# A two-layer hybrid step in split fp32: the high part against 512 columns per tile from layer 1's first down product on

## The chip, the cores and the metric

The kernel runs on 1 core of one Trainium2 chip. The metric is the device time of one execution in microseconds (us); before the change the median of 3 runs is 2454.88 us (2451.24 to 2457.85). PE is the matmul engine (PEld its weight loads), ACT the scalar engine, DVE the vector engine, POOL the general engine, SP the engine that issues most DMAs here.

## What is computed

Two layers over 128 context and 128 latent tokens (256 columns in all) with width 2048. Cut to what matters here:

```python
def trunk_layer(x, mod, ...):
    shift1, scale1, gate1, shift2, scale2, gate2 = mod      # mod = silu(c) @ w_mod + b_mod
    q_r, k_r, v_r, g_r, q_a, k_a, v_a = project(modulate(x, shift1, scale1), w_in_l)
    ...                                                     # retention heads and attention heads
    x = x + gate1 * (jnp.concatenate([y_r, y_a], axis=-1) @ w_out_l)
    x = x + gate2 * conv_ffn(modulate(x, shift2, scale2), w_up_l, conv_w_l, conv_b_l, w_down_l)

def conv_ffn(h, w_up_l, conv_w_l, conv_b_l, w_down_l):      # D_FF = 5632, conv of width 3 over tokens
    up = jnp.pad(h @ w_up_l, ...)
    u = conv_b_l + sum(up[:, j:j + T] * conv_w_l[j] for j in range(3))
    gate, val = jnp.split(u, 2, axis=-1)
    return (jax.nn.silu(gate) * val) @ w_down_l
```

All weights are fp32 in DRAM and every one is read once.

## The kernel before

**Tiles, pieces, items.** Activations lie transposed, features on partitions, the 256 tokens in the free dimension. A weight is cut into tiles of 128 by 128; eight tiles are a piece, and the kernel is a list of 768 pieces in a fixed order: layer 0's input projection (pieces 0 to 87), its output projection `out` (88 to 119), then three thirds of the gated MLP, each an `up` product and a `down` product (120 to 383); layer 1 the same from 384, with its `out` at 472, its first `up` at 504 and its first `down` at 568. The thirds hold 16, 16 and 12 chunks of 128 hidden features. A group is four output chunks `n` of 128 features; an `up` chunk needs 16 tiles, a `down` chunk 16, 16 or 12.

**Split products.** To keep fp32 accuracy with single-pass fp32r matmuls, each weight piece is split on ACT into a rounded high part `hi` (L478) and on DVE into the rest `lo` (L479), three pieces ahead (`LOOK`), and each activation likewise: of the 512 columns of an `hT` chunk or of a `ypair` chunk the first 256 are the high part, the last 256 the low part. `triple` (L644 to L648) then makes three matmuls of 256 columns per tile into one accumulator: `hi` by high, `hi` by low, `lo` by high. Each matmul instruction loads its own weights.

**Accumulators.** `ps_m` holds five PSUM banks of 512 columns. Two output chunks share a bank (columns 0 to 255 and 256 to 511). When a pair is done, `evac` passes the bank on: for `up` to `ffn_pair` (convolution, silu, product, split; one stage per piece later), for `down` and `out` to ACT (times the gate, L726) and DVE (added to `xT`, L728). The last two chunks of `out` and of the last `down` take a bank each and go through `evac_one` (L700). In the first group of each `down` the four chunks are interleaved over all but the last four feature chunks.

**Modulation.** The vectors `shift`, `scale`, `gate` are products of `w_mod` (1 MB loads into the three `vec` buffers, in the order in which they are used) with two condition columns. Some are made on PE (`mod`, L402, four plain fp32 matmuls per load; `modq`, L388, one quarter of a vector in four loads), others as dot products on DVE (`dot`, L411, two instructions of 2.28 us per load). A plan made before the code is written out puts them behind pieces: `quota` with its `knots` for `mod`, `room`, `due` and `plan` for `dot`. Before, neither comes before piece 48 (`ahead`). Loads of pieces (`raw`, 512 KB, L335, five buffers) and of modulation (`vec`, L325) share SP's queue in order of their need.

**Side work.** The attention and retention heads of a layer are generators that `step_side` advances by one step behind each piece (and in the middle of it where two wait). An attention group (`q_task`) runs scores, softmax (`norm`), transposes on PE (`flip`, L857) and the product with the values (`mix`, L870) for three batches of heads.

## Time and profile before

| what | value |
|---|---|
| median of 3 runs | 2454.88 us (2451.24 to 2457.85) |
| the profiled execution, time | 2457.62 us |
| its span on the core | 2455.8 us, mean granted clock 0.99 |
| PE busy | 97% of the span, 19694 matmuls |
| PEld, DVE, ACT busy | 93%, 75%, 49% |
| DMA | 619 MB, mean 252 GB/s |

PE is busy in all but a few of the 40 slices. A matmul's start and end overlap with its neighbours', so its mean length (280 ns) is not what it costs; the distance from one start to the next is.

### The profile page before, as it was taken

The page shows a single profiled execution, that of the slowest core. Times are in us where ns is not written, and L with a number is a line of the kernel's source. Part 1 is how long each engine was busy: PE and PEld are TensorE (multiplying, and loading weights), DVE is VectorE, ACT ScalarE, POOL GpSimd, SP SyncE. Part 2 cuts the span into 40 slices and gives each one's busy share as a digit, 9 for nine tenths or more (in the row PEclk, how much of TensorE's full clock was granted, in tenths as well). Part 3 has the DMA queues.
Part 4 walks back from the last instruction along what each step waited for, and adds up shares of the span by engine and source line. Part 5 has one row for each costly group of instructions (what it writes and reads, how often), then busy time and mean ns, then how long its engine had stood idle before and what let it go on. Part 6 is the DMA issues. An engine that isn't in the chain of part 4 may idle for free.

```text
span 2455.8 us, 47593 instructions
## 1 busy us (share of the span) xinstructions
PE 2383.7 (97%) x19694; PEld 2287.2 (93%) x19694; DVE 1853.3 (75%) x2461; ACT 1203.4 (49%) x1901; POOL 21.7 (1%) x29
## 2 busy tenths in 40 slices
PE   6999999999999999999999999999999999999998
PEld 3888888889999999999989899999999999999997
DVE  4557778769998899889987777797896466655665
ACT  3534434455544455445556444456554445544554
POOL 0000000000000000000000000000000000000000
PEclk8999999999999999999999999999999999999999
DMA  9987788976888777777775677877676666666653
GB/s 377 350 310 258 274 308 327 372 252 230 277 277 283 264 254 271 274 268 256 254 285 191 231 275 280 298 269 257 227 253 187 183 188 186 186 182 186 188 181 121
DMA packets 146569, 619.46 MB, mean 252 GB/s; under 512 B 16304, under 2 KB 22448, under 8 KB 121392
## 3 DMA queue, kind: packets, MB, share of 16 engines
q1 hardware_dynamic: 138816, 605.24, 71.5%
q10 hardware_dynamic: 7536, 11.19, 1.3%
q8 instruction: 154, 2.52, 0.4%
q14 instruction: 63, 0.52, 0.1%
HBM read 611.64 MB, written 4.72 MB: 251 GB/s over the span
## 4 chain that ended last, share of the span: by engine, by line
PE 85%; DVE 8%; DMA 3%; issue 2%; ACT 2%; ACTq 0%; POOL 0%; DVEq 0%; SPq 0%; POOLq 0%
PE acc L646 27%; PE acc L648 26%; PE acc L647 26%; DVE lo L479 2%; DVE hua L411 2%; PE md L388 2%; DMA vec<-in_w_modq 2%; DMA vec<-in_w_mod 1%; PE md L402 1%; ACT hi L478 1%; ACT pr L842 0%; DMA vec<-in_w_dot 0%; DVE grp L640 0%; PE aux L870 0%; PE aux L443 0%
## 5 line engine op out<-in xcount | busy, mean ns | idle before, releaser
L646 PE MATMUL acc<-hT,hi 128*128 128x256 f32 x4224 | 1201.4, 284 | 5.9 <-ACT hT L573 5.9
L479 DVE TENSOR_TENSOR lo<-raw,hi 128x1024 fp32r<-128x1024 f32 x768 | 934.9, 1222 | 349.8 <-ACT hi L478 348.4
L648 PE MATMUL acc<-hT,lo 128*128 128x256 f32 x4224 | 1182.2, 280 | 2.4 <-DVE lo L479 2.4
L647 PE MATMUL acc<-hT,hi 128*128 128x256 f32 x4224 | 1182.2, 280 | 0.6 <-DVE hT L578 0.6
L478 ACT CAST hi<-raw 128x1024 fp32r<-128x1024 f32 x768 | 803.4, 1050 | 628.5 <-PE acc L647 543.9
L646 PEld LDWEIGHTS acc<-hT,hi 128*128 128x128 f32 x4224 | 795.9, 188 | 33.7 <-issue 15.3
L648 PEld LDWEIGHTS acc<-hT,lo 128*128 128x128 f32 x4224 | 796.0, 188 | 3.8 <-DVE lo L479 3.6
L647 PEld LDWEIGHTS acc<-hT,hi 128*128 128x128 f32 x4224 | 794.0, 188 | 4.2 <-issue 1.9
L648 PE MATMUL acc<-ypair,lo 128*128 128x256 f32 x1920 | 544.1, 283 | 2.3 <-DVE lo L479 2.3
L646 PE MATMUL acc<-ypair,hi 128*128 128x256 f32 x1920 | 546.1, 284 | 0.0
L647 PE MATMUL acc<-ypair,hi 128*128 128x256 f32 x1920 | 543.8, 283 | 0.0
L411 DVE SCALAR_TENSOR_TENSOR hua<-vec,cbc 128x2048 bf16<-128x2048 f32 x208 | 475.2, 2284 | 5.8 <-DMA vec<-in_w_dot 5.8
L646 PEld LDWEIGHTS acc<-ypair,hi 128*128 128x128 f32 x1920 | 369.0, 192 | 9.3 <-issue 6.7
L648 PEld LDWEIGHTS acc<-ypair,lo 128*128 128x128 f32 x1920 | 369.0, 192 | 3.0 <-DVE lo L479 3.0
L647 PEld LDWEIGHTS acc<-ypair,hi 128*128 128x128 f32 x1920 | 369.1, 192 | 0.1
L726 ACT ACTIVATE gx<-acc,modT 128x128 f32<-128x128 f32 x240 | 68.6, 369 | 113.5 <-PE acc L648 113.5
L728 DVE TENSOR_TENSOR xT<-gx,xT 128x512 f32<-128x512 f32 x60 | 41.5, 691 | 71.0 <-ACT gx L726 70.9
L755 DVE SCALAR_TENSOR_TENSOR cv<-acc,cst,cv 128x254 f32<-128x254 f32 x176 | 84.8, 482 | 6.2
L746 ACT ACTIVATE cv<-acc,cst 128x256 f32<-128x256 f32 x176 | 89.3, 558 | 0.0
L388 PE MATMUL md<-vec,sc 128*32 128x512 f32 x448 | 62.2, 664 | 26.5 <-DMA vec<-in_w_modq 26.5
L753 DVE SCALAR_TENSOR_TENSOR cv<-acc,cst,cv 128x254 f32<-128x254 f32 x176 | 83.5, 475 | 0.0
L759 ACT ACTIVATE cv<-cv 128x256 f32<-128x256 f32 x88 | 36.4, 414 | 71.3 <-DVE cv L755 71.2
(130 smaller groups left out, 893.9 us busy)
## 6 DMA issues: line engine op xcount, KB each, us to landing
raw<-in_w_up SPq DMA_DIRECT2D x352, 512.0 KB, 4.3
vec<-in_w_dot SPq DMA_DIRECT2D x104, 1024.0 KB, 5.3
raw<-in_w_in SPq DMA_DIRECT2D x176, 512.0 KB, 5.4
raw<-in_w_down SPq DMA_DIRECT2D x176, 512.0 KB, 4.2
vec<-in_w_modq SPq DMA_DIRECT2D x56, 1024.0 KB, 7.4
vec<-in_w_mod SPq DMA_DIRECT2D x32, 1024.0 KB, 8.3
raw<-in_w_out SPq DMA_DIRECT2D x64, 512.0 KB, 5.9
xT<-in_xT ACTq DMA_DIRECT2D x2, 1024.0 KB, 9.5
```

What stands on the lines that cost most here:

```text
L388: nc.tensor.matmul(md[0][32 * j:32 * j + 32, :], sc[:, 2 * kc:2 * kc + 32], t[:, 512 * i:512 * i + 512], start=kc < 4, stop=kc >= 12)
L411: nc.vector.scalar_tensor_tensor(hua.rearrange("p c t -> p (c t)").bitcast(BF16), raw[key], 1.0, acc[:, k, :], op0=ALU.mult, op1=ALU.mult, ...
L478: nc.scalar.copy(hi, r)
L479: nc.vector.tensor_tensor(lo, r, hi.bitcast(F32), op=ALU.subtract)
L646: nc.tensor.matmul(out, hi, src[:, 0:256], start=first, stop=False, skip_group_check=True)
L647: nc.tensor.matmul(out, hi, src[:, 256:512], start=False, stop=False, skip_group_check=True)
L648: nc.tensor.matmul(out, lo, src[:, 0:256], start=False, stop=last, skip_group_check=True)
L726: nc.scalar.activation(tv[:, i, P * s:P * s + P], pv[:, i, P * s:P * s + P], AF.Copy, scale=modT[l][:, v, nt + i, s:s + 1])
L728: nc.vector.tensor_tensor(xT[:, nt:nt + 2, :], tv, xT[:, nt:nt + 2, :], op=ALU.add)
L746: nc.scalar.activation(t, src, AF.Identity, bias=C("convb", l * 2 * FC + f, 1), scale=w)
L753: nc.vector.scalar_tensor_tensor(t[:, :, 1:P], src[:, :, 0:P - 1], w[0], t[:, :, 1:P], op0=ALU.mult, op1=ALU.add)
L755: nc.vector.scalar_tensor_tensor(t[:, :, 0:P - 1], src[:, :, 1:P], w[2], t[:, :, 0:P - 1], op0=ALU.mult, op1=ALU.add)
```

## The change

Three edits.

1. `halves(j, g)` holds for the `up` and `down` groups of layer 1 from its first `down` on (pieces 568 to 767, that is 896 `up` tiles and 704 `down` tiles). There a tile takes two matmuls in place of three: `hi` by all 512 columns (high and low activations) into a whole bank, and `lo` by the high 256 columns into the bank's first half. An output chunk thus has a bank of its own, and when it is complete ACT copies the bank's second half to SBUF (`tb`) and DVE adds the first half to it (`r`); `evac` and `evac_one` then read `r`.
2. Layer 0's plan: `mod` may start at piece 43 and has a knot at `out`'s start, three quarters of 32 loads by then; `dot` may also stand in pieces 27 to 31 and 43 to 47.
3. In `q_task` the first batch's `flip` has a step of its own behind the second batch's `norm`.

```diff
-    knots = [(ahead, 0), (gstart["up", 0] - 6, 2 * MU), (gstart["kv", 1] + 16, 2 * MU),
+    knots = [(ahead - 5, 0), (gstart["out", 0], 3 * MU // 2), (gstart["up", 0] - 6, 2 * MU), (gstart["kv", 1] + 16, 2 * MU),
...
-        if j >= ahead and not ends:
-            room[j] = DSHARE[g["kind"]] if j >= gstart["out", 0] else 0.3
+        if not ends:
+            if j >= gstart["out", 0]:
+                room[j] = DSHARE[g["kind"]]
+            elif j >= ahead or j >= 2 * WIDE and j % (2 * WIDE) >= 11:
+                room[j] = 0.3
...
-        elif issued[0] + 1 < quota(j, knots):
+        if j >= ahead - 5 and not hs and issued[0] + 1 < quota(j, knots):
...
+            if halves(j, g):
+                src = Y(kc) if g["kind"] == "down" else hT[:, kc, :]
+                if cur["ps"][n] is None:
+                    cur["ps"][n] = ps_m.tile([P, 512], F32, tag="m", name="acc")
+                out = cur["ps"][n]
+                c[n] += 1
+                nc.tensor.matmul(out, hi_t[j][:, P * i:P * i + P], src, start=c[n] == 1, stop=False,
+                                 skip_group_check=True)
+                nc.tensor.matmul(out[:, 0:256], lo_t[j][:, P * i:P * i + P], src[:, 0:256], start=False,
+                                 stop=c[n] == nk, skip_group_check=True)
+                if c[n] == nk:
+                    fin.append((n, out, single))
+                continue
...
-            if single:
+            if halves(j, g):
+                if n % 2 == 0:
+                    cur["r"] = tp.tile([P, 512], F32, tag="t2", name="r", bufs=4)
+                r = cur["r"][:, 256 * (n % 2):256 * (n % 2) + 256]
+                t = tp.tile([P, 256], F32, tag="t1", name="tb", bufs=3)
+                nc.scalar.copy(t, ps[:, 256:512])
+                nc.vector.tensor_tensor(r, ps[:, 0:256], t, op=ALU.add)
+                if single:
+                    evac_one(g, g["ns"][n], r)
+                elif n % 2 == 1:
+                    evac(gi, g, n, cur["r"])
+            elif single:
...
+    def halves(j, g):
+
+        return g["l"] == DEPTH - 1 and g["kind"] in ("up", "down") and g["first"] >= gstart["down", DEPTH - 1]
...
-        for step in ([(scores, 0)], [(scores, 1)], [(norm, 0)], [(norm, 1), (flip, 0)], [(scores, 2), (mix, 0)],
+        for step in ([(scores, 0)], [(scores, 1)], [(norm, 0)], [(norm, 1)], [(flip, 0)], [(scores, 2), (mix, 0)],
                      [(flip, 1), (norm, 2)], [(mix, 1)], [(flip, 2)], [(mix, 2)]):
```

On PE, at the second feature chunk of layer 1's first `down` group (the numbers behind the names tell banks and weight pieces apart), before:

```order
L646 MATMUL acc_21300<-ypair_19772,hi_21229 128x256
L647 MATMUL acc_21300<-ypair_19772,hi_21229 128x256
L648 MATMUL acc_21300<-ypair_19772,lo_21230 128x256
L646 MATMUL acc_21307<-ypair_19772,hi_21229 128x256
L647 MATMUL acc_21307<-ypair_19772,hi_21229 128x256
L648 MATMUL acc_21307<-ypair_19772,lo_21230 128x256
```

and at the same place now:

```order
L614 MATMUL acc_21300<-ypair_19772,hi_21229 128x512
L616 MATMUL acc_21300<-ypair_19772,lo_21230 128x256
L614 MATMUL acc_21303<-ypair_19772,hi_21229 128x512
L616 MATMUL acc_21303<-ypair_19772,lo_21230 128x256
L614 MATMUL acc_21306<-ypair_19772,hi_21229 128x512
L616 MATMUL acc_21306<-ypair_19772,lo_21230 128x256
L614 MATMUL acc_21309<-ypair_19772,hi_21229 128x512
L616 MATMUL acc_21309<-ypair_19772,lo_21230 128x256
```

Each tile has two instructions in place of three, and the group's four chunks lie in four banks instead of two; the whole program has 1600 matmuls fewer.

On SP, the loads issued towards the end of layer 0's `out` product (`raw` are weight pieces, `vec` modulation loads, by the DRAM array that they come from), before:

```order
L325 DMA vec<-in_w_mod 128x2048 x2
L335 DMA raw<-in_w_out 128x1024
L335 DMA raw<-in_w_up 128x1024
L325 DMA vec<-in_w_dot 128x2048
L335 DMA raw<-in_w_up 128x1024 x2
L325 DMA vec<-in_w_modq 128x2048 x3
L335 DMA raw<-in_w_up 128x1024
L325 DMA vec<-in_w_modq 128x2048
L335 DMA raw<-in_w_up 128x1024 x4
```

and now:

```order
L329 DMA vec<-in_w_dot 128x2048
L329 DMA vec<-in_w_mod 128x2048
L339 DMA raw<-in_w_out 128x1024
L329 DMA vec<-in_w_mod 128x2048
L339 DMA raw<-in_w_out 128x1024 x2
L339 DMA raw<-in_w_up 128x1024
L329 DMA vec<-in_w_modq 128x2048
L339 DMA raw<-in_w_up 128x1024 x2
L329 DMA vec<-in_w_modq 128x2048 x2
L339 DMA raw<-in_w_up 128x1024
L329 DMA vec<-in_w_modq 128x2048
```

The last `dot` load ahead of the first `modq` load has moved in front of the last two `mod` loads, and the first `modq` load stands two weight pieces sooner.

On ACT, in layer 0's first attention group (`pr` are the exponentials, `pt` the copy behind the transposes of `flip`, `ypair` the result of `mix`), before:

```order
L478 CAST hi<-raw 128x1024
L840 ACTIVATE st<-st 128x2
L842 ACTIVATE pr,st<-aux,st 128x256 x2
L478 CAST hi<-raw 128x1024
L859 COPY pt<-aux 128x512
L840 ACTIVATE st<-st 128x2
L842 ACTIVATE pr,st<-aux,st 128x256 x2
L876 CAST ypair<-aux 128x2x128 x2
```

and now:

```order
L482 CAST hi<-raw 128x1024
L872 ACTIVATE st<-st 128x2
L874 ACTIVATE pr,st<-aux,st 128x256 x2
L482 CAST hi<-raw 128x1024
L891 COPY pt<-aux 128x512
L482 CAST hi<-raw 128x1024
L872 ACTIVATE st<-st 128x2
L874 ACTIVATE pr,st<-aux,st 128x256 x2
L908 CAST ypair<-aux 128x2x128 x2
```

One weight piece's cast now stands between the first `flip` and the third batch's scores; the attention group has ten steps in place of nine.

## Rows read from the trace of the kernel before

**Rows 1.** the page of before: busy us, share of the span, instruction counts

```profile
PE 2383.7 (97%) x19694; PEld 2287.2 (93%) x19694; DVE 1853.3 (75%) x2461; ACT 1203.4 (49%) x1901; POOL 21.7 (1%) x29
```

**Rows 2.** stretches: length, busy (xcount) of PE, PEld, DVE, ACT; clock, DMA

```profile
390.00:520.00 130.00, 118.43 (x933) 101.42 (x932) 93.49 (x118) 52.10 (x94) 1.38 (x2) 0.96 0.93 352
1871.70:2441.80 570.10, 570.10 (x4802) 569.98 (x4800) 330.34 (x409) 285.32 (x435) 0.00 (x0) 1.00 0.58 179
1875.00:1960.00 85.00, 85.00 (x710) 85.00 (x710) 43.47 (x43) 38.97 (x60) 0.00 (x0) 1.00 0.60 182
1970.00:2050.00 80.00, 80.00 (x682) 80.00 (x681) 49.94 (x69) 40.35 (x56) 0.00 (x0) 1.00 0.62 188
```

**Rows 3.** groups of 1871.7 to the end: names, shapes, xcount | busy, mean ns

```profile
L646 PE MATMUL acc<-hT,hi 128*128 128x256 f32 x896 | 250.9, 280 | 0.0
L479 DVE TENSOR_TENSOR lo<-raw,hi 128x1024 fp32r<-128x1024 f32 x197 | 241.1, 1224 | 192.4 <-ACT hi L478 192.4
L478 ACT CAST hi<-raw 128x1024 fp32r<-128x1024 f32 x197 | 206.7, 1050 | 240.0 <-PE acc L647 210.6 <-ACT cv L746 24.5 <-issue 5.0
L646 PE MATMUL acc<-ypair,hi 128*128 128x256 f32 x704 | 199.2, 283 | 0.0
...
L753 DVE SCALAR_TENSOR_TENSOR cv<-acc,cst,cv 128x254 f32<-128x254 f32 x58 | 27.5, 475 | 0.0
L760 DVE TENSOR_TENSOR cv<-cv 128x256 f32<-128x256 f32 x29 | 12.1, 419 | 0.0
```

**Rows 4.** PE timeline, 12 matmuls apart, granted clock 0.5

```profile
517.53 0.41 PE L647 MATMUL acc<-hT,hi 128*128 128x256 f32 x1
...
520.09 0.41 PE L647 MATMUL acc<-hT,hi 128*128 128x256 f32 x1
```

**Rows 5.** PE timeline, nine matmuls apart, right after a wait

```profile
586.45 0.28 PE L647 MATMUL acc<-hT,hi 128*128 128x256 f32 x1
...
587.47 0.28 PE L647 MATMUL acc<-hT,hi 128*128 128x256 f32 x1
```

**Rows 6.** PE timeline, plain fp32 products of the side work at half clock

```profile
238.75 1.91 PE L828 MATMUL aux<-KT,grp 128*128 128x256 f32 x4
240.45 1.11 PE L870 MATMUL aux<-pt,vtok 128*128 128x512 f32 x2
```

**Rows 7.** PE timeline, the same products at full clock

```profile
1353.79 1.03 PE L828 MATMUL aux<-KT,grp 128*128 128x256 f32 x4
1354.65 1.02 PE L870 MATMUL aux<-pt,vtok 128*128 128x512 f32 x2
```

**Rows 8.** ACT by line: the one copy of this size out of a bank

```profile
L529 ACT COPY rb<-aux 128x256 f32<-128x256 f32 x5 | 1.9, 373 | 5.2 <-PE aux L528 5.2
```

**Rows 9.** what PE waited for, 200 to 520: us in total, times, longest

```profile
PE md L388 <- DMA vec<-in_w_modq: 6.1, 1, 6.1
PE md L402 <- DMA vec<-in_w_mod: 3.0, 2, 2.8
PE aux L857 <- ACT pr L842: 2.6, 1, 2.6
PE aux L857 <- DVE pr L850: 1.5, 2, 0.9
```

**Rows 10.** what PE waited for, 1230 to 1600

```profile
PE aux L857 <- DVE pr L850: 2.2, 1, 2.2
PE aux L857 <- ACT pr L842: 1.6, 1, 1.6
```

**Rows 11.** PE timeline, the wait at the end of the out product

```profile
495.09 1.93 PE L388 MATMUL md<-vec,sc 128*32 128x512 f32 x8 [6.09 <-DMA vec<-in_w_modq]
...
497.33 0.41 PE L647 MATMUL acc<-ypair,hi 128*128 128x256 f32 x1
...
499.68 0.41 PE L646 MATMUL acc<-ypair,hi 128*128 128x256 f32 x1
```

**Rows 12.** SP timeline, loads issued ahead of that wait

```profile
486.63 8.30 SPq L325 DMA_DIRECT2D vec<-in_w_modq  x3
```

More of the change, by code (lines that the diff above doesn't have):

```diff
@@ L149, in body @@
         gstart.setdefault((g["kind"], g["l"]), j)
+        g.setdefault("first", j)
     def mod_event():
@@ L600, in emit_piece @@
         fin = []
+        c = cur["n"]
         for i, (n, kc) in enumerate(p["tiles"]):
-            c = cur["n"]
             single = g["ns"][n] >= KC - 2 and last_add(g)
+            if halves(j, g):
[11 more added lines that the diff above has]
+                continue
             b = n if single else n // 2 * 2
```

## The prediction, made before the result was known

> **What bounds the kernel now.** I read the busy line first: PE is busy 97% of the span and has as many weight loads as matmuls [rows 1]; the load of its own weights goes with every matmul. Then the stretches: from 1871.7 to 2441.8, where layer 1's first down product begins and the last matmul ends, PE is busy for all 570.1 us at full clock, while DVE and ACT are busy 330 and 285 us and DMA 0.58 [rows 2]. So in the part that the change rewrites, the end is set by the distance of one matmul from the next, and by nothing else. That distance comes from the counts: 682 in 80 us of an up product and 710 in 85 us of a down product, two or three of each begun before the stretch, are 0.118 and 0.120 us [rows 2]. With the counts of the two forms [rows 3], 3 x (896 x 0.1178 + 704 x 0.120) = 570.0 us: the whole stretch. The mean length of 280 ns is that of overlapping instructions and costs nothing.
>
> The early part, layer 0's input and out products, is another regime: between 390 and 520 PE is busy 118 of 130 us with DMA at 0.93 [rows 2], and it waits by name for modulation loads and for the softmax [rows 9].
>
> **What a 512-column matmul costs.** This decides nearly all. At half clock (1.2 GHz) twelve matmuls take 2.56 us, 0.2133 each [rows 4]: exactly one column per cycle for 256 columns, nothing on top. At full clock (2.4 GHz) the same stream is 0.1067, but they start 0.118 or 0.120 apart: 11 to 13 ns on top. What adds them? Right after a wait nine of them went at 0.113 each [rows 5]. One and the same instruction at 0.113, 0.118 and 0.120 speaks against a slower rate per column, and for a hand-over between the weight load and the stream, which at full clock are about as long as each other. The trace has matmuls with a stream twice as long that load their own weights too: plain fp32 passes of the attention's scores take (240.45 - 238.75) / 4 = 0.425 at half clock [rows 6] and 0.215 at full clock [rows 7], only 2.5 ns above the half. Their stream is as long as that of 512 single-pass columns. So I take 0.215 for the new `hi` matmul; the `lo` matmul behind it is again 256 columns long with the next weight load beside it, and keeps 0.118 or 0.120.
>
> A tile then takes 0.333 us in up products (0.353 before) and 0.335 in down products (0.360 before). 896 x 0.020 + 704 x 0.025 = 35.5 us; I take 35 off the 570.
>
> Bounds: if the 11 and 13 ns belong to every fp32r matmul whatever its length, one of them is saved per tile: 896 x 0.0111 + 704 x 0.0133 = 19 us. If they are a rate per column, nothing is saved. The nearest rows, at the same stream length, are the 0.215 ones, so I take the upper end.
>
> The Trainium skill (page "TensorE: Matmul & The Clock Gate", section "Wait — 56ns, not 53.3ns?") has a fixed 2.5 ns per warm matmul at every length; by it alone 1600 matmuls fewer save 4 us. The 256-column matmuls here don't follow it, with 11 to 13 ns [rows 2]; the plain fp32 passes do, with 0.215 [rows 7].
>
> **What the halves add.** The 26 groups concerned have 104 output chunks; each now needs one ACT copy of 128x256 out of a bank, 0.373 us [rows 8], and one DVE addition, between 0.419 and 0.475 us [rows 3]. That is 39 us on ACT and 44 to 49 on DVE, beside PE: ACT goes to some 324 of 535 us and DVE to 377 of 535. Both stay below PE. They queue in order, though: behind each copy stands the next `hi` cast (1.05 us), behind each addition the next `lo` (1.22) [rows 3]. Those are made three pieces ahead, about 8 us, so 0.4 us in front of them is hidden by that lead; ACT's casts already wait 211 us for PE to give buffers back [rows 3]. Without the cover each chunk would cost PE 0.8 us.
>
> Banks: a chunk holds one of five. Between two uses of a bank lie four other chunks, 16 to 21 us, against a hand-back of copy, addition and at most one cast and one `lo` before them, 3 us. The tightest place is the first group of each down product, which wants four banks within its first four tiles: the third of those was closed 16 tiles (5.3 us) earlier, still enough. So I put no wait there.
>
> The end of the program: behind the last matmul the last chunk's copy and addition come in front of the gated sum, 0.37 + 0.42 = 0.8 us, all of it on the path.
>
> **What the early edits move.** PE's largest single wait, 6.1 us at 489 to 495, is for a `modq` load [rows 9, 11]. SP issued the three such loads over 8.3 us from 486.6 on [rows 12], since the three buffers were full of the last two `mod` loads and of a dot that was placed right there. Now that dot's buffer comes free three pieces (8.6 us) before the first `modq` is used, and four `mod` loads and a dot unit have left the out stage for pieces 29 to 47. After that wait the clock is half up to 499.9: (499.68 - 497.33) / 11 = 0.214 per matmul [rows 11], 4.8 us of work at half speed, so 2.4 us lost. I take 5 of the wait and those 2.4, and 2.5 of the 3.0 us for `mod` loads [rows 9]. The moved units issue their loads past some twenty weight pieces on SP, and their DVE halves stand in front of `lo` splits; in the opening that DMA is busy too, so I allow 2 us back.
>
> The separate step for `flip` gives the softmax half a piece to a piece more (1.4 to 2.8 us) before PE needs it. Its waits are 2.6 + 1.5 in layer 0 and 2.2 + 1.6 in layer 1 [rows 9, 10], the longest two with a spell of half clock behind them. I take 5 us, and 1 back, because all later side steps move back a step and the last heads come nearer to the out product. Together the early edits give 12 us; bounds 22 (all of these waits and their clock) and 3 lost (they come back elsewhere).
>
> **The sum.** 2457.6 of the profiled execution - 35 + 0.8 - 12 = 2411. That execution is 2.7 above the median of 2454.9, so the time to compare is 2409.
>
> **Rivals.**
> (a) The added ns belong to each fp32r matmul: 19 in place of 35, time 2425. For it: at 256 columns no row is below 0.113. Against it: 0.425 and 0.215 [rows 6, 7].
> (b) They stay with the columns, as a rate, and only the instruction's own part of 2.5 ns goes: 0 to 4 us saved in place of 35, time 2440 to 2444, above 2447 if the early edits give less than 5 to 9 us. Against it: 0.113 beside 0.120 [rows 2, 5], and 0.2133 at half clock [rows 4].
> (c) The early edits only move their waits: 2421.
> (d) Slower, by banks. PE, with a whole bank per chunk, waits for its next bank. After a wait the granted clock was half [rows 11], so a wait of 2.2 us costs some 4 with the slow spell behind it. Of 104 hand-backs 12 such would use up the 47 us of gain; from there on the kernel is slower, and 40 of them give 2409 + 160 = 2569. The banks' 16 us against 3 speak against it, and so does that PE has no wait in this stretch at present, where the pair's bank is held twice as long.
> The Trainium skill (same page, section "A second HAM failure mode: psum-queue depth-cycling") speaks against this change in just that way: cycling through banks at 512 columns let PE idle often and the clock swing. The row behind 495 shows such a swing after a wait, but no run here yet shows one from banks.
>
> **Chances.** Forecast 0.70 (2409, own range 2399 to 2419), (a) 0.15, (b) 0.05, (c) 0.06, (d) 0.04. The range for 8 in 10 reaches from 2398 (all early waits gone) to 2428 (past (a)) and leaves out (b), (d) and the edges. A measurement of this kernel can tell about 0.3%, 7 us, from no change. Faster by more: the forecast, (a), (c) and part of (b), 0.93; within: the rest of (b), 0.03; slower: (d), 0.04.
>
> **What would show it.** In the new trace the `hi` rows of 512 columns followed by `lo` rows 0.215 later and the next `hi` 0.118 to 0.120 after that; 0.224 to 0.227 would be (a), 0.235 and more (b). From the first down product to the last matmul 535 us, PE busy for all of it, no PE wait for a `tb` or `r` instruction. The last matmul to the end 14.8 in place of 14. No 6 us wait before `modq` at the end of layer 0's out product, and shorter waits at `flip`. I am wrong if PE shows gaps at the start of a chunk, or if the first 1871.7 us are not 8 or more shorter.

## The result and the profile after

| | before | after |
|---|---|---|
| median, runs on one chip | 2453.59 us (2451.24 to 2457.85) | 2431.24 us (2429.58 to 2437.47) |
| ratio, 95% interval | | 0.9904 [0.9884, 0.9924] |
| profiled execution: time, span | 2457.62, 2455.8 us | 2432.38, 2430.6 us |

The change is faster by 22 us, 0.96%. The forecast of 2409 (2398 to 2428) had the sign right and twice the gain. The gain is not where it was forecast, either: of the 25.2 us between the two spans the rewritten stretch gave 6.5 and the part ahead of it 19.7, and the tail took 1 back. These are two single executions, 3 us further apart than the medians; what the medians give each part stands with the experiments.

The page's busy line of after:

```profile
PE 2371.9 (98%) x18094; PEld 2204.5 (91%) x18094; DVE 1892.6 (78%) x2565; ACT 1242.9 (51%) x2005; POOL 27.5 (1%) x29
```

1600 matmuls fewer than in [rows 1], as the diff says; PE's busy time fell by 12 us alone.

Stretches of after: length, busy time (xcount) of PE, PEld, DVE, ACT and POOL, then granted clock, DMA share, GB/s. The first is from layer 1's first `down` matmul to the start of the last matmul, the answer to the 570.1 us of [rows 2], the second a piece of a down product:

```profile
1852.04:2415.54 563.50, 563.50 (x3201) 491.16 (x3199) 370.33 (x512) 321.72 (x536) 0.00 (x0) 1.00 0.57 181
1860.00:1945.00 85.00, 85.00 (x483) 73.74 (x482) 48.28 (x56) 45.71 (x79) 0.00 (x0) 1.00 0.57 185
```

PE is busy for all of it at full clock, as before, and DVE and ACT stay far below it. PE is the bound, and it takes 563.6 us with the last matmul, where 535 were forecast. What a matmul costs there is seen in the PE timeline of after, in a down product (start, length, line, tiles):

```profile
1900.17 0.28 PE L616 MATMUL acc<-ypair,lo 128*128 128x256 f32 x1
1900.29 0.40 PE L614 MATMUL acc<-ypair,hi 128*128 128x512 f32 x1
1900.53 0.28 PE L616 MATMUL acc<-ypair,lo 128*128 128x256 f32 x1
1900.65 0.40 PE L614 MATMUL acc<-ypair,hi 128*128 128x512 f32 x1
1900.88 0.28 PE L616 MATMUL acc<-ypair,lo 128*128 128x256 f32 x1
1901.00 0.40 PE L614 MATMUL acc<-ypair,hi 128*128 128x512 f32 x1
```

From a 512-column start to the next 256-column start it is 0.23 to 0.24 us, and back 0.12. Over all 1600 tiles of this trace the tile takes 0.3533 in up products (0.3533 before: nothing gained) and 0.351 in down products (0.360 before): 896 x 0.3533 + 704 x 0.351 = 563.6. The forecast had 0.333 and 0.335.

The 0.351 is no price of a tile, but a mean of two. The row of 1860 to 1945 above, in the stretch's first down product, has 483 matmuls in 85 us; the same length of the second down product has ten more:

```profile
2125.00:2210.00 85.00, 85.00 (x493) 74.95 (x492) 51.15 (x59) 46.32 (x79) 0.00 (x0) 1.00 0.58 191
```

From the starts, the 256 tiles of the second down product take 0.3467 each and all other tiles 0.3533; each product keeps its price from its first tile to its last.

Groups of 1852 to the end in after (names, shapes, xcount | busy, mean ns | idle before):

```profile
L614 PE MATMUL acc<-hT,hi 128*128 128x512 f32 x896 | 316.7, 396 | 0.0
...
L640 DVE TENSOR_TENSOR r<-acc,tb 128x256 f32<-128x256 f32 x104 | 43.8, 424 | 81.4 <-ACT tb L639 81.4
```

The 104 additions cost 0.424 us each, as worked out, and no matmul of the stretch waits: the idle column of `L614` is zero.

Now the part ahead. What PE waited for from 200 to 520 us in after:

```profile
PE md L406 <- DMA vec<-in_w_mod: 3.3, 3, 1.6
PE aux L968 <- DVE rk L954: 2.8, 3, 2.0
PE aux L889 <- ACT pr L874: 2.7, 3, 1.5
```

The 6.1 us for `modq` of [rows 9, 11] are gone; the sum for `mod` loads is no smaller, it sits elsewhere. Here are two neighbouring stretches of layer 0's `out` product, pieces 96 to 112 and 112 to 118, of before and then of after (columns as above):

```profile
417.30:474.90 57.60, 54.60 (x450) 47.70 (x449) 46.55 (x50) 23.97 (x42) 0.00 (x0) 1.00 0.94 358
474.90:504.00 29.10, 23.01 (x172) 19.57 (x172) 19.23 (x23) 10.19 (x19) 0.00 (x0) 0.88 1.00 399
```

```profile
418.50:469.80 51.30, 50.41 (x419) 46.95 (x418) 43.72 (x48) 22.33 (x36) 0.00 (x0) 1.00 0.92 357
469.80:490.70 20.90, 20.90 (x174) 18.32 (x173) 14.51 (x17) 10.09 (x19) 0.00 (x0) 1.00 0.87 341
```

57.6 to 51.3: 31 matmuls have left for earlier pieces, and 2 us of waiting with them. 29.1 to 20.9: the wait and the half clock (0.88) are gone.

The end: `tb` and `r` stand behind the last matmul (2415.39) as forecast,

```profile
2415.70 0.37 ACT L639 COPY tb<-acc 128x256 f32<-128x256 f32 x1 [3.81 <-PE acc L616]
2416.11 0.42 DVE L640 TENSOR_TENSOR r<-acc,tb 128x256 f32<-128x256 f32 x1 [3.11 <-ACT tb L639]
```

and from its end to the end of the span it is 14.9 us in place of 14.

### The profile page after: what moved, and what is told of

The parts are those of the page before. It is cut to its first block, busy times and chain, and to the rows that moved or that the text cites. A ratio compares the mean times of both kernels' runs of the same rounds, so it can differ in the third digit from the quotient of the medians.

```text
span 2430.6 us, 44608 instructions
## 1 busy us (share of the span) xinstructions
PE 2371.9 (98%) x18094; PEld 2204.5 (91%) x18094; DVE 1892.6 (78%) x2565; ACT 1242.9 (51%) x2005; POOL 27.5 (1%) x29
## 4 chain that ended last, share of the span: by engine, by line
PE 87%; DVE 6%; DMA 3%; issue 2%; ACT 2%; SPq 0%; DVEq 0%; POOLq 0%; ACTq 0%; POOL 0%
PE acc L674 20%; PE acc L676 19%; PE acc L675 19%; PE acc L614 15%; PE acc L616 8%; DVE lo L483 2%; PE md L392 2%; DVE hua L415 2%; DMA vec<-in_w_modq 1%; DMA vec<-in_w_mod 1%; PE md L406 1%; ACT hi L482 0%; ACT pr L874 0%; PE aux L902 0%; PE aux L447 0%
## 5 line engine op out<-in xcount | busy, mean ns | idle before, releaser
L674 PE MATMUL acc<-hT,hi 128*128 128x256 f32 x3328 | 950.5, 286 | 5.9 <-ACT hT L577 5.9
L675 PE MATMUL acc<-hT,hi 128*128 128x256 f32 x3328 | 931.8, 280 | 0.6 <-DVE hT L582 0.6
L674 PEld LDWEIGHTS acc<-hT,hi 128*128 128x128 f32 x3328 | 626.9, 188 | 35.4 <-issue 17.0
L675 PEld LDWEIGHTS acc<-hT,hi 128*128 128x128 f32 x3328 | 625.8, 188 | 4.5 <-issue 1.9
L674 PE MATMUL acc<-ypair,hi 128*128 128x256 f32 x1216 | 346.0, 285 | 0.0
L675 PE MATMUL acc<-ypair,hi 128*128 128x256 f32 x1216 | 344.0, 283 | 0.0
L614 PE MATMUL acc<-hT,hi 128*128 128x512 f32 x896 | 316.7, 396 | 0.0
L614 PE MATMUL acc<-ypair,hi 128*128 128x512 f32 x704 | 247.2, 396 | 0.0
L674 PEld LDWEIGHTS acc<-ypair,hi 128*128 128x128 f32 x1216 | 233.2, 192 | 6.8 <-issue 5.0
L676 PEld LDWEIGHTS acc<-ypair,lo 128*128 128x128 f32 x1216 | 233.2, 192 | 3.0 <-DVE lo L483 3.0
L675 PEld LDWEIGHTS acc<-ypair,hi 128*128 128x128 f32 x1216 | 233.3, 192 | 0.1
L614 PEld LDWEIGHTS acc<-hT,hi 128*128 128x128 f32 x896 | 168.4, 188 | 40.6
L614 PEld LDWEIGHTS acc<-ypair,hi 128*128 128x128 f32 x704 | 132.1, 188 | 31.5
```

Source lines behind the costliest of these rows:

```text
L614: nc.tensor.matmul(out, hi_t[j][:, P * i:P * i + P], src, start=c[n] == 1, stop=False, skip_group_check=True)
L674: nc.tensor.matmul(out, hi, src[:, 0:256], start=first, stop=False, skip_group_check=True)
L675: nc.tensor.matmul(out, hi, src[:, 256:512], start=False, stop=False, skip_group_check=True)
L676: nc.tensor.matmul(out, lo, src[:, 0:256], start=False, stop=last, skip_group_check=True)
```

## The experiments

"Lead" of a piece below is how much sooner its first matmul starts than in before, from the starts in the two traces.

**One edit at a time.** Four kernels: edit 1 alone, edit 2 alone, edit 3 alone, and 2 with 3. The edits are those of the diff above; an edit left out reads as before, and without edit 1:

```diff
     def halves(j, g):
-        return g["l"] == DEPTH - 1 and g["kind"] in ("up", "down") and g["first"] >= gstart["down", DEPTH - 1]
+        return False
```

> The change's first edit alone: layer 1's high part against 512 columns, layer 0's plan and the flip step as before. In the trace of the changed kernel the stretch from the first down product to the last matmul took 563.5 us in place of 570.1, all of the gain in the down products, and the end behind it 15.0 in place of 14.0. Theory (the two parts of the change are independent of each other): 5 to 6 us faster than the kernel before (0.998). Rival (the stretch was faster in that one execution only, or the copies and additions cost elsewhere): no difference, 0 within 2 us.

> Layer 0's plan alone (mod and dot units sooner), with three matmuls per tile and the flip step as before. Theory: it takes away the 6.1 us wait for modq at the end of layer 0's out product and the half-clock spell behind it and a part of the waits for mod loads, and gives back some 5 us where the first mod units now come (pieces 44 to 52): 8 to 13 us faster in all, all of it before piece 120, nothing in layer 1. Rival (the flip step did it): less than 4 us.

> The separate step for the first flip alone, the plan and the matmuls as before. Theory: it takes away the waits for the softmax in layer 1 (2.2 and 1.6 us, and 1.7 us of half clock behind the first), 5 to 6 us there between pieces 404 and 416, and 2 to 4 us in layer 0 (2.6 and 1.5 us with 1.7 of half clock, less what its later steps cost): 6 to 10 us faster. Rival (the waits only move to later side steps): 0 to 2 us.

> The change without its first edit: three matmuls per tile throughout, layer 0's plan and the flip step as in the changed kernel. Theory: 19 to 20 us faster than before (0.992), which is most of the change; the rest of it, the halves, is worth 5 to 6. Rival: the halves are worth more than the one trace shows, and this is less than 15 faster.

| kernel | median us | ratio to before | lead at piece 88 | 112 | 120 | 404 | 428 |
|---|---|---|---|---|---|---|---|
| halves alone (`e1_halves_only`) | 2447.40 | 0.9963 [0.9951, 0.9975] | | 0.8 | 1.3 | -1.7 | 0.5 |
| plan alone (`e2_plan_only`) | 2449.34 | 0.9970 [0.9958, 0.9982] | -7.3 | -3.0 | 5.4 | 7.5 | 9.3 |
| flip alone (`e3_flip_only`) | 2459.15 | 1.0013 [1.0004, 1.0022] | -8.6 | -8.0 | -8.5 | -6.9 | -1.0 |
| plan and flip (`e4_plan_and_flip`) | 2442.38 | 0.9942 [0.9930, 0.9954] | -2.8 | 5.7 | 14.1 | 16.4 | 21.9 |
| all (after) | 2431.24 | 0.9904 [0.9884, 0.9924] | -2.5 | 4.9 | 13.3 | 13.9 | 19.7 |

Halves give some 8 us, plan and flip 13 to 14; the two early edits are the larger part of the change. Three of the four theories missed: plan alone (8 to 13 expected) gains 6, flip alone (6 to 10 gained expected) loses 4, and plan and flip (19 to 20 expected) stay under the 15 us that the rival named; halves alone are 2 to 3 us better than the 5 to 6 expected. The leads come from single traces and overrate the early edits: the profiled execution of plan and flip is 5.6 us below the median of its runs, that of before 4 above. Nine traces with the layer 0 of the change have leads of 10 to 14 at piece 120, so a lead is good to some 4 us.

Plan and flip are no sum: apart they give 6 gained and 4 lost, together 13 to 14. The separate step for `flip` costs 8.5 us in layer 0 with the old plan (piece 120) and gains 8.7 there on top of the new one (5.4 to 14.1). In layer 1 pieces 404 to 428 take 91.8 to 92.6 us in twelve traces with the step, 95.6 and 95.9 in halves alone and plan alone, which lack it, and 97.7 in before. So the step gains 3.5 to 4 us there; the other 2 of the 5.5 to 6 in the table are a spell of half clock that only before's trace has. Here are pieces 404 to 406 of before, of plan alone and of flip alone (columns as above):

```profile
1343.78:1355.11 11.33, 9.12 (x60) 8.61 (x59) 10.57 (x18) 5.06 (x10) 0.00 (x0) 0.85 0.57 185
```

```profile
1336.11:1345.90 9.79, 7.60 (x61) 7.08 (x59) 9.58 (x17) 5.06 (x10) 0.00 (x0) 1.00 0.51 145
```

```profile
1350.43:1356.45 6.02, 6.02 (x55) 6.02 (x53) 5.93 (x9) 4.48 (x9) 0.00 (x0) 1.00 0.51 143
```

Before and plan alone have the same 2.2 us wait for `pr`, and only in the first does the clock fall behind it.

In the run of flip alone PE waited from 200 to 520 us for

```profile
PE aux L965 <- DVE rk L951: 6.8, 4, 2.0
PE md L389 <- DMA vec<-in_w_modq: 6.4, 1, 6.4
PE aux L886 <- ACT pr L871: 4.8, 2, 3.6
```

so both the retention's `rk` and the softmax's `pr` come later than in before, and `modq` as late.

**What a 512-column matmul depends on.** First the number of columns. In layer 1's groups one matmul of w columns stands in place of the tile's pair, w by group (so these groups' sums are not the model's):

```diff
-                nc.tensor.matmul(out, hi_t[j][:, P * i:P * i + P], src, start=c[n] == 1, stop=False,
...
+                    nc.tensor.matmul(out[:, 0:w], hi_t[j][:, P * i:P * i + P], src[:, 0:w], start=c[n] == 1,
```

> From layer 1's first down product on, four down groups and eight up groups make one matmul per tile, of hi by the first N columns (the low part of the weights is left out there, and the sums are not those of the model): N 512, 384, 256, 128 in the down groups and 512, 448, 384, 320, 256, 192, 128, 64 in the up groups; each still loads its own weights. Theory (a rate: an fp32r column costs 0.46 ns whatever the length): the starts are 0.234, 0.206, 0.176, 0.147, 0.118 us apart for 512 to 256 columns, a line through zero, and a floor set by the weight load at 0.107 to 0.113 for 192 and fewer. Rival (a fixed cost per matmul, at 2.4 columns per ns): 0.224, 0.198, 0.171, 0.144, 0.118, a line with 11 ns at zero. Second rival (a hand-over that only the balance of load and stream at 256 causes): 0.216, 0.189, 0.162 for 512 to 384.

Medians of the distance between starts, worked out from the trace: 0.2275 us for 512 columns from `ypair` and 0.2295 from `hT`, 0.201 for 448, 0.174 for 384, 0.147 for 320, 0.118 to 0.119 for 256. Below 256 little is saved: 192 and 128 columns take 0.109 to 0.116 in the few rows at full clock. Most of these groups, and all of the one with 64 columns, ran at half clock, since PE waits for `hi` there; a matmul then takes 0.213, whether of 192, 128 or 64 columns. At one column per cycle of the full clock 512 columns are 0.2133 and 256 0.1067: 14 to 16 ns above that at 512, 13.5 to 14.5 at 320 to 448, 11 to 12 at 256. Theory (a rate) and second rival (0.216 at 512) fall. It is nearly a fixed price per matmul, as in rival (a) of the prediction, and not the 2.5 ns that I had taken for 512.

Then the operands (again sums that aren't the model's): constant weights and fixed moving tiles, in bf16 and in fp32r.

```diff
+                        nc.tensor.matmul(out[:, 0:w], bconst[:, 0:P], mconst[:, 0:w], start=False, stop=last, ...
+                        nc.tensor.matmul(out[:, 0:w], wconst, hT[:, 0, 0:w], start=False, stop=last, ...
```

> In seven up groups of layer 1's second third the operands are replaced (all but each output chunk's first tile, so the sums are not the model's): one group with constant weights but 512 and 256 columns as now; two with bf16 weights and a bf16 moving operand of 512 columns, one with 256; two with fp32r of 512 columns from one fixed address, one with 256. Loads and splits go on beside it. Theory (the moving operand's 4 bytes per column cannot be read at one column per cycle): bf16 takes 0.216 for 512 columns and 0.107 to 0.113 for 256, fp32r stays at 0.23 and 0.118 whatever its address. Rival (the array or the bank's write side limits): bf16 takes 0.234 too. Second rival (the place of the operand in memory): the fixed address changes fp32r's 0.231 to 0.240.

Its PE timeline, rows of 15 matmuls with one length each (the length is 14 distances and one matmul):

```profile
1971.86 3.41 PE L631 MATMUL acc<-hua 128*128 128x512 bf16 x15
...
1997.96 1.81 PE L631 MATMUL acc<-hua 128*128 128x256 bf16 x15
...
2018.95 3.59 PE L635 MATMUL acc<-hT 128*128 128x512 f32 x15
...
2047.34 1.96 PE L635 MATMUL acc<-hT 128*128 128x256 f32 x15
```

bf16: (3.41 - 0.38) / 14 = 0.216 and (1.81 - 0.27) / 14 = 0.110. fp32r (printed as f32): (3.59 - 0.39) / 14 = 0.229 and (1.96 - 0.28) / 14 = 0.120. The array, the banks, the number of weights and the columns are the same; the type differs, and with it the bytes of an element and the buffers that they are read from. The Trainium skill (page "TensorE: Matmul & The Clock Gate", section "Wait — 56ns, not 53.3ns?") gives a warm matmul a fixed 2.5 ns above its columns: the bf16 rows agree (0.216, 0.110), the fp32r rows don't (11 to 16 ns).

Does the neighbourhood matter? In the next kernel the last 72 pieces have neither loads nor splits, and constant weights:

```diff
-        while nload["main"] < len(units) and held["main"] < RAWB and nload["mod"] >= MU // 2:
+        while nload["main"] < QUIET and held["main"] < RAWB and nload["mod"] >= MU // 2:
...
-        while nsplit[0] < min(n, len(pieces)):
+        while nsplit[0] < min(n, QUIET):
```

> From layer 1's last up product on (the last 72 pieces) nothing is loaded and nothing is split any more; the matmuls are the same 512 and 256 columns with constant weights (the sums are not the model's). DVE and ACT have only the evacuation left, DMA nothing. Theory (a rate of fp32r itself): a tile keeps its 0.351 to 0.353 us. Rival (the writes of DVE, ACT and DMA into SBUF beside it slow the reading): a tile falls towards 0.216 + 0.109 = 0.325 us in that stretch.

In that stretch of the run (columns as above)

```profile
2180.00:2400.00 220.00, 220.00 (x1261) 192.87 (x1260) 70.30 (x144) 64.57 (x160) 0.00 (x0) 1.00 0.04 12
```

DMA is down to 0.04 and DVE to a third, and a tile still takes 230 + 117 = 347 ns in up and 235 + 118 = 353 ns in down products. Both are prices that products of the same order have with loads and splits beside them, too (table by product below), and far from 325. So the rival falls: the extra isn't made by the writes beside PE.

**Is it the alternation?** In the changed kernel's trace the long matmul takes 0.234 us, 5 to 7 ns more than the 0.2275 to 0.2295 among equals. So: the eight long ones of a piece first, the eight short ones behind.

```diff
-        fin = []
+        fin, low = [], []
...
-                nc.tensor.matmul(out[:, 0:256], lo_t[j][:, P * i:P * i + P], src[:, 0:256], start=False,
-                                 stop=c[n] == nk, skip_group_check=True)
+                low.append((out, i, src, c[n] == nk))
...
+        for out, i, src, last in low:
+            nc.tensor.matmul(out[:, 0:256], lo_t[j][:, P * i:P * i + P], src[:, 0:256], start=False,
+                             stop=last, skip_group_check=True)
```

> The changed kernel, but within each piece of the halves' groups the eight 512-column matmuls come first and the eight 256-column ones behind them; nothing else differs. In the run of mixed column counts a 512-column fp32r matmul among its like took 0.227 to 0.2295 us from start to start and a 256-column one 0.118; in the changed kernel, where the two alternate, the longer takes 0.234 and the pair 0.351 to 0.353. Theory: the alternation of lengths costs the longer one some 6 us per thousand. Then 1600 x (0.352 - 0.347) = 8 to 10 us go: the stretch from layer 1's first down product to the last matmul 554 to 556 us in place of 563.6, the time some 8 to 10 us below the changed kernel. Rival: the extra belongs to the change of weights or to the bank written, not to the neighbour's length: the pair stays at 0.351 to 0.353 and the time stays within 2 us of the changed kernel.

> The changed kernel itself, for a comparison on the same chip and against the same runs of before: 0.99 of the time before, by either theory.

By length 2424.32 us, ratio 0.9877 [0.9863, 0.9892]; the changed kernel beside it 2429.38, 0.9905 [0.9887, 0.9924]. By length is the fastest version here, 5 us below the change. Its stretch and two pieces of its PE timeline:

```profile
1853.95:2408.85 554.90, 554.77 (x3201) 488.09 (x3199) 369.39 (x512) 314.86 (x537) 0.00 (x0) 1.00 0.57 183
```

```profile
1901.30 2.00 PE L614 MATMUL acc<-ypair,hi 128*128 128x512 f32 x8
1903.14 1.11 PE L632 MATMUL acc<-ypair,lo 128*128 128x256 f32 x8
1904.09 2.00 PE L614 MATMUL acc<-ypair,hi 128*128 128x512 f32 x8
```

(1904.09 - 1901.30) / 8 = 0.349 for a tile of a down product. Over all tiles (mean distances of the two matmuls added):

| execution | up tile, us | down tile, us | stretch, us |
|---|---|---|---|
| before | 0.3533 | 0.360 | 570.1 |
| after, its first trace | 0.3533 | 0.351 | 563.6 |
| after, beside by length (`e10_changed_again`) | 0.3508 | 0.349 | 560.1 |
| by length (`e8_by_length`) | 0.3447 | 0.349 | 554.8 |

554.8 us is inside the 554 to 556 expected, and the rival (no difference) falls. But the theory isn't shown by it. Beside its neighbour of the same chip only up tiles gain, 896 x 0.0061 = 5.5 us, 3.7 ns of the 6.1 in the short matmul and not in the long one; a down tile costs 0.349 in either order. The gain in time is 5 and not 8 to 10 for the same reason. One and the same alternating program differs by 3.5 us from execution to execution; the two kernels by length (`e8_by_length`, `e11_by_length_late_mod`) both take 554.8.

The mean distances product by product show why, in ns per tile, from layer 1's first `down` product to its last (its first `up` product lies ahead of the stretch):

| execution | down 1 | up 2 | down 2 | up 3 | down 3 |
|---|---|---|---|---|---|
| before | 360.0 | 353.3 | 360.0 | 353.3 | 360.0 |
| after, its first trace | 353.3 | 353.3 | 346.7 | 353.3 | 353.3 |
| after again (`e10_changed_again`) and halves alone (`e1_halves_only`) | 346.7 | 348.9 | 353.3 | 353.3 | 346.7 |
| by length (`e8_by_length`, `e11_by_length_late_mod`) | 349.2 | 344.8 | 349.2 | 344.8 | 349.1 |

In turn, a product has one of three prices, 346.7, 348.9 or 353.3, and keeps it from its first tile to its last; the same product has another in another execution. At 346.7 the alternation costs nothing: equals among equals add up to as much (0.2295 + 0.118 or 0.2275 + 0.119 us), and a sorted down tile takes more. So what costs is not the neighbour's length as such, but the price that a product falls into at its start; in the traces the up products never had the lowest one, except in the quiet run. What sets it, no run here shows. Sorted, the price is the same in each trace. It depends on the place in the chunk there: the eight short matmuls of an up chunk's first piece take (1.11 - 0.28) / 7 = 0.119, those of its second (1.07 - 0.28) / 7 = 0.113 us, with no wait before either.

```profile
1986.50 1.07 PE L632 MATMUL acc<-hT,lo 128*128 128x256 f32 x8
1987.40 1.99 PE L614 MATMUL acc<-hT,hi 128*128 128x512 f32 x8
1989.23 1.11 PE L632 MATMUL acc<-hT,lo 128*128 128x256 f32 x8
```

**Is it the weight load?** Two constant fp32r matmuls per tile, with 128, 64 or 32 columns of weights:

```diff
+                        nc.tensor.matmul(out[0:m, 0:w], hT[:, 15, 0:m], hT[:, 0, 0:w], start=False,
+                                         stop=last and r == 1, skip_group_check=True)
```

> In layer 1's groups 4 to 11 of the halves' stretch the tiles of the products are replaced by two fp32r matmuls of constant operands each, with weights of 128, 64 or 32 columns and 512, 256 or 384 moving columns (so these groups compute nothing of the model). It asks what the 11 to 15 ns above the column count of an fp32r matmul are. If they are the hand-over from the weight load, they shrink with the weights: with 32 columns of weights 0.216 us for 512 moving columns and 0.109 for 256, as bf16 had. If they belong to the fp32r stream, the distance stays at 0.227 to 0.2295 and 0.118 whatever the weights. 384 moving columns: 0.174 with 128 columns of weights by either, 0.162 with 32 by the first.

PE timeline, rows of 30 with 128 and 32 columns of weights, at 512 and at 256 moving columns:

```profile
1942.14 6.97 PE L626 MATMUL acc<-hT 128*128 128x512 f32 x30
...
1999.80 7.11 PE L626 MATMUL acc<-hT 128*32 128x512 f32 x30
...
2029.14 3.76 PE L626 MATMUL acc<-hT 128*128 128x256 f32 x30
...
2059.94 3.69 PE L626 MATMUL acc<-hT 128*32 128x256 f32 x30
```

(6.97 - 0.40) / 29 = 0.227 and (7.11 - 0.39) / 29 = 0.232; 0.120 and 0.118; with 384 columns 0.173 for either. With 64 columns of weights the medians are 0.229 and 0.113. The differences follow no order of the width, and a quarter of the weights saves nothing near the 11 ns: the hand-over from the weight load, on which the forecast built, is not it. What in the fp32r stream costs the 11 to 16 ns stays open; no kernel here takes it apart further.

**Which part of the plan.** Modulation loads later, on top of by length:

```diff
-    knots = [(ahead - 5, 0), (gstart["out", 0], 3 * MU // 2), ...
+    knots = [(ahead + 8, 0), (gstart["out", 0], 3 * MU // 2), ...
```

> The run before (by length), with modulation loads for PE from piece 56 on in place of 43. In the trace of the changed kernel PE falls back by 7.7 us between pieces 44 and 56, where the first of these units now stand, and gets some of it back only by piece 100. Theory: these units at the end of the kv product are too early, and with them back at 56 the 5 to 8 us are kept: 4 to 8 us below the run by length alone. Rival: the same units have to be squeezed in later, in front of the out product, and the wait for loads of the quarters at its end comes back: no gain, or a loss of up to 6 us.

2435.22 us, 0.9917 [0.9900, 0.9934]: 11 us slower than by length alone. The lead is -15.7 at piece 88 and 0.8 at 120. The theory falls. The 8 us that the early units seemed to cost were a dip: in after the lead is -7.6 at piece 52 and -0.9 at 58 again, since these units' own work only stands earlier. The rival had the sign, but not the place: the 8 us between pieces 112 and 120 are kept, the loss is all ahead of piece 88.

Then the plan's two halves, each with flip: the `room` lines alone, and the `knots` and `mod_event` lines alone.

> Before, with the separate step for flip and only the dots' half of the new plan (dots also in pieces 27 to 31 and 43 to 47; the mod loads where they were; no halves). In the order the dot that stood between the last two mod loads and the first modq load (behind piece 114) is at pieces 111 and 112. Theory: that dot alone made the 6.1 us wait for modq, so the wait is under 1.5 us here and the half-clock spell behind it goes: some 8 us between pieces 112 and 120, as in the run of plan and flip. And if flip alone lost its 8.5 us in layer 0 to dots that stand in front of the softmax on DVE, moving the dots mends that as well: 2442 to 2447. Rival: it takes the earlier mod loads too; then the wait stays over 3 us and the time is 2450 or more.

> The other half: before, with the separate step for flip and the mod loads from piece 43 on with the knot at the out product; the dots where they were; no halves. The order behind piece 114 is then that of before, two mod loads and a dot ahead of the first modq load. Theory: the wait of some 6 us for modq is still there, with its half clock, and the time is 2451 to 2458. Rival (the mod loads are what filled the buffers): the wait goes and the time is 2442 to 2447.

| kernel | median us | ratio | lead at 88 | 112 | 120 | 428 |
|---|---|---|---|---|---|---|
| dots and flip (`e12_dots_and_flip`) | 2450.95 | 0.9979 [0.9969, 0.9988] | -10.7 | -7.8 | -2.1 | 5.8 |
| mod loads and flip (`e13_mods_and_flip`) | 2452.54 | 0.9988 [0.9977, 0.9998] | -7.8 | 0.7 | 1.4 | 7.3 |

PE's wait for `modq`, 480 to 520 us, with the dots moved and with the mod loads moved:

```profile
PE md L392 <- DMA vec<-in_w_modq: 2.1, 1, 2.1
```

```profile
PE md L389 <- DMA vec<-in_w_modq: 5.5, 1, 5.5
```

Mod loads alone leave it, as expected (2451 to 2458), with a granted clock of 0.66 from 493 to 501. The dot in front of `modq` makes 4 of the 6 us (under 1.5 us left were expected), and its half clock is gone too: 1.00 from 498 to 506. The last 2 us take both halves. The second part of the theory missed: with the dots moved flip still loses 8 us by piece 112, and the time is 2451, not 2442 to 2447. With the earlier mod loads the lead at 112 is 0.7 in place of -8.0, but they don't mend what is lost by piece 88 (-7.8): their gain comes behind it, where their units stood. Only flip with both halves of the plan loses little by piece 88 (-2.8). Why stays open.

**The price elsewhere, and the cover.** By length in the up and down groups of both layers; the first two up groups of a layer, 128 tiles each time, are written by another function (`duo_piece`) and keep three matmuls per tile, so it is 1664 up tiles more and not the 1920 of the expectation:

```diff
-        return g["l"] == DEPTH - 1 and g["kind"] in ("up", "down") and g["first"] >= gstart["down", DEPTH - 1]
+        return g["kind"] in ("up", "down")
```

> The run by length with halves() true for every up and down group of both layers: 1920 up and 704 down tiles more. By the prices of the run by length (0.3447 in place of 0.3534, 0.349 in place of 0.360) PE has 1920 x 0.0087 + 704 x 0.011 = 24 us less to do. Theory one: PE is the bound there as well, and the time is 2398 to 2406. Rival: in these stretches DVE is busy 0.89 to 0.94 of the time already (173 of 185 us from 515 to 700), and 168 more additions of some 0.45 us are 76 us; DVE then is the bound, lo splits come late, PE waits for lo, and the gain is under 8 us or becomes a loss of up to 30.

2450.07 us, 0.9980 [0.9970, 0.9990]: 26 us slower than by length in the last 200 pieces. Layer 0's MLP (pieces 120 to 380) in after, then in this kernel:

```profile
502.70:1251.00 748.30, 744.31 (x6253) 742.04 (x6253) 684.74 (x830) 384.91 (x575) 0.00 (x0) 1.00 0.74 260
```

```profile
502.70:1265.80 763.10, 738.59 (x4300) 641.06 (x4300) 722.09 (x949) 413.58 (x695) 0.00 (x0) 1.00 0.74 254
```

DVE goes from 0.92 to 0.95 of the time, PE's idle time from 4 to 24.5 us, and most of that is one wait:

```profile
PE acc L632 <- DVE lo L483: 15.2, 22, 1.9
```

The rival holds: where DVE has no room, the additions make the `lo` splits late. Against the 19 us that the prices give layer 0 (1280 x 0.0087 + 704 x 0.011) it is 15 us longer.

## Why the prediction was wrong

- **What bounds.** Right: PE waits for nothing in the rewritten stretch, and its price per tile is the stretch. With quiet neighbours it keeps to two of the values that it has with busy ones.
- **The 512-column matmul: the step that failed.** "So I take 0.215 for the new `hi` matmul" rested on plain fp32 passes with a stream of the same length [rows 6, 7]. The runs show that the type decides: 0.216 in bf16, 0.227 to 0.233 in fp32r among its like. The argument for it, that 0.113, 0.118 and 0.120 for one instruction speak for a hand-over from the weight load, fell with the narrow weights, and 0.113 is no sign of a wait before: sorted, every second piece of an up product has it. At this point it was rival (a), "the added ns belong to each fp32r matmul", whose tile is 0.342 and 0.3467; by length the runs come close to that (0.3447 and 0.349). By the signs that the prediction set, 0.224 to 0.227 for (a) and 0.235 and more for (b), the long matmul of the change lies between, at 0.230 to 0.237 by product.
- **What no rival had.** In the order of the change, 512 and 256 columns in turn, a tile has one of three prices, product by product, and the up products got the two upper ones: an up tile takes 0.351 to 0.353 in the mean, all but what it took before, and in down products the merger saves 9 to 11 ns. The lowest, 0.3467, is (a)'s price of a down tile. So the first term is 6.5 to 10 us in place of 35, between (a), 19, and (b), 0 to 4.
- **The halves' own work.** Right in size (0.424 per addition, DVE 370 us of 563) and right that it is hidden there. Layer 0 in the last experiment shows the cover gone.
- **Banks, rival (d).** No wait. The Trainium skill's rule on cycling through banks at 512 columns (same page, section "A second HAM failure mode: psum-queue depth-cycling") isn't seen here: granted clock 1.00 for all of the 563.5 us.
- **The tail.** 0.8 forecast, 0.9 to 1 measured.
- **The early edits: near their size, but not for the reasons given.** Plan and flip gain 13 to 14 us by the medians, against the 12 of the forecast; the pair of traces gives 19.7, inside the bound of 22, with 2 of them the half clock that only before's trace has behind its wait in layer 1. By the leads of after: `modq` and its half clock 8.4 (112 to 120; forecast 7.4, and the dot does make most of it); flip in layer 1 3.5 to 4, about the waits of [rows 10], and in this pair the spell of half clock; 2.5 lost by piece 88 (forecast 2). What the sum lacked is pieces 96 to 112, 6.3 us: the moved mod units take their matmuls along, to where PE is short of work anyway. I had counted a unit's wait and its loads, not its own PE time. What I put down instead, 2.5 us less waiting for `mod` loads, only moved (3.0 to 3.3). That flip would gain in layer 0 by itself was wrong: it loses 8.5 there under the old plan. That the term came out near its size is in part luck.
- **The sum.** By the medians the halves give 8 us (halves alone) in place of 34, the early edits 13 to 14 in place of 12. So nearly all of the miss is the first term's, and 2431 lies just outside the range, between (a) and (b).

## What to carry to other kernels

Take the price of a matmul from rows of the same type; a row of equal stream length in another type is another instruction. Where a merger leaves two lengths in turn, try them sorted by length: here that gave 5 us more. A unit moved out of a full stage takes its own engine time along, and two moves in one stage are to be tried together, since their effects don't add. What two traces differ by is not yet what a change is worth: here 6 us of an early part of 19.7 weren't in the medians.

## What the runs showed of the hardware

- A matmul with its own weight load, full clock: bf16 0.110 us for 256 columns and 0.216 for 512; fp32r 0.113 to 0.120 and, among its like, 0.227 to 0.233; fp32r of 192 and 128 columns 0.109 to 0.116.
- The fp32r extra doesn't fall with the weights' width (128 to 32 columns), with fixed in place of changing addresses (0.227 to 0.229), or with DVE, ACT and DMA nearly idle beside it.
- fp32r of 512 and 256 columns in turn: 0.3467, 0.3489 or 0.3533 us a pair, the same through a whole product of 192 to 512 tiles, and 560.1 to 563.6 us for one and the same stretch in different executions; sorted by length 0.345 in up and 0.349 in down products and 554.8 both times. What sets the price of a product stays open.
- Behind one and the same 2.2 us wait of PE the mean granted clock was 0.85 in one execution and 1.00 in another.
